# Feed-forward units of a hybrid decoder block on one core: from three seven-product and three plain units to four and one

## The chip, the cores and the metric

The kernel runs on one NeuronCore of a Trainium2 chip. The metric is the device time of one execution in microseconds; the median of three runs is shown. PE is TensorE (matmuls, transposes), DVE VectorE, ACT ScalarE, POOL GpSimd, SP the engine that issues most transfers.

## The reference

One decoder layer on 256 tokens of width 1024, all in float32. The change touches the feed-forward half alone:

```python
h = rms_norm(x, norm_ffn_pre_g[l])
f = (jax.nn.silu(h @ w_gate[l]) * (h @ w_up[l])) @ w_down[l]     # D_FF = 2816
x = x + rms_norm(f, norm_ffn_post_g[l])
```

## The kernel before

**Precision.** A float32 product is made of three matmuls of fp32r operands: each operand is split into a high part (`whi`: a ScalarE copy, L188) and a low part (`wlo`: source minus high, VectorE, L191), and `mm3` (L220 to L222) does high x high, high x low, low x high. Each weight tile (128 x 1024 elements, two rows of k for 512 columns) has one high and one low buffer out of a ring of five (`WB`), so the split of a tile waits until TensorE is through with the tile five places earlier.

**The feed-forward half.** The 2816 hidden columns are 22 chunks of 128 (`NFF`). Chunks 0 to 3 are computed first (`nat`). The other 18 go by `UNITS`:
- A plain unit R has two chunks: 8 x 2 x 3 matmuls of 512 columns (gate 256, up 256), two PSUM banks, 4 weight tiles. It ends with one group of four transposes.
- A seven-product unit W has four chunks. Two token halves t, two halves of k and the two matrices gate and up form 2 x 2 blocks, which are multiplied with seven products in place of eight (names "11", "T1", "T2", "22", "T3", "21", "T4"; each 4 x 3 = 12 matmuls of 512 columns, in two halves, one per weight tile). Its weights are sums: T1 and T3 are loaded and then a second matrix is added to them by an accumulating transfer on POOL's queue (L166); T2 and T4 are sums on VectorE (`job_add`, L271). The activations' sums (`S`, `s_step`) are made once. After its products, small VectorE and ScalarE operations put the two hidden tiles together (`q1` to `q7`).

**Transposes.** `f_T` (L997) turns a hidden tile (128 tokens x 512) into four 128 x 128 transposes in one PSUM bank, tag "t" (L1000), then copies the high part out (`fT`, ScalarE, L1005) and the low part (VectorE, L1007). The bank is free when the low part is done.

**Down terms.** For each chunk f a down-projection term `("d", f)` adds to the four output banks: 9 matmuls of 512 columns and 6 of 256, with one split tile of w_down (`dr`). A unit's slots are followed by the terms of the unit before it (`units_before`). The last four terms are the tail; their tiles lie in pages (`wextra`).

**What sets the order.** TensorE and SP take the order of the code; ScalarE, VectorE and POOL too in this half. `run` goes through the list of slots; before each slot it emits the split jobs that the slots ahead need (`granules_ahead`: up to four tiles, at most six slots), then the slot's matmuls, then what follows the slot. So in the lists of ScalarE and VectorE the splits for later slots stand between the small operations. Weights of W units lie in 12 pages (`free`), loaded in the order of first use (`page_order`) as soon as a page is released; other weights in a ring of seven raw buffers (`RB`). Each load is one instruction on SP's list.

```python
UNITS = [("R", 4), ("W", 6), ("R", 10), ("W", 12), ("R", 16), ("W", 18)]
head = slots_of("21", "b", A(0, 1), True, True, q2)
body = slots_of("11", "a", ...), [... ("T2", "a", ...), ("T1", "b", ...), ("T3", "a", ...), ("22", "b", ...), ("T4", "a", ...)]
return head + body[0], body[1], [f_T({1: lambda: st["f1"]}, f0, 4)]      # f_T of the first half ends body[1]
slots += a + zs[0:2] + (zs[2:] + b if i < len(UNITS) - 1 else b + zs[2:])
```

## Time and profile before

| | |
|---|---|
| median of 3 runs | 383.99 us (383.75 to 384.27) |
| profiled execution | 384.85 us, its span 383.1 us |
| TensorE matmul busy | 369.6 us, 96% of the span, 2212 instructions |
| TensorE weight loads busy | 322.8 us, 84% |
| VectorE busy | 298.1 us, 78%, 540 instructions |
| ScalarE busy | 234.2 us, 61%, 431 instructions |
| GpSimd busy | 47.1 us, 12% |
| transfers | 77.08 MB, mean 201 GB/s; mean granted TensorE clock 0.997 |

Matmuls overlap, so the distance from start to start tells what one costs, and a busy share near 100% does not say that no time is lost. A row of a timeline has start, duration, engine, line, operation, output<-inputs and, in brackets, the idle time before it with what released the engine. L numbers are lines of the kernel before.

### The profile page before, as it was taken

To read this page: it belongs to the slowest core of one execution; us is meant where nothing else is said; L and a number is where in the kernel's file an instruction comes from. 1 tells how busy PE (TensorE), PEld (TensorE's weight loads), DVE (VectorE), ACT (ScalarE), POOL (GpSimd) and SP (SyncE) were. 2 spreads that over 40 slices of the span, in tenths; PEclk is the share of its full clock that TensorE was granted. 3 is DMA by queue.
4 is the path that set the end of the run, shared out by engine and by line. 5 is a ranking of instruction groups with operands and counts; after the bars stand their busy time and mean duration, and the time that the engine had idled before them with its cause. 6 is when DMAs were issued, how large, how long until landed. Compare 5 with 4: busy or idle time off the path is not lost.

```text
span 383.1 us, 6164 instructions
## 1 busy us (share of the span) xinstructions
PE 369.6 (96%) x2212; PEld 322.8 (84%) x2212; DVE 298.1 (78%) x540; ACT 234.2 (61%) x431; POOL 47.1 (12%) x63
## 2 busy tenths in 40 slices
PE   6999999999999999999999999999999999999893
PEld 4799989999999999898888888887888877887683
DVE  3699797899978757789669886887588776877944
ACT  3985576778665865565467555684546853567721
POOL 0099600000001000000004010112001120000000
PEclk9999999999999999999999999999999999999998
DMA  6988646253654563577349999999958899300003
GB/s 204 388 255 322 198 137 201 70 164 113 215 153 128 193 192 125 188 215 248 107 120 318 299 401 274 386 282 360 297 147 221 239 347 300 129 0 0 3 0 110
DMA packets 42752, 77.08 MB, mean 201 GB/s; under 512 B 3281, under 2 KB 15586, under 8 KB 42722
## 3 DMA queue, kind: packets, MB, share of 16 engines
q1 hardware_dynamic: 39458, 70.40, 54.9%
q0 software_dynamic: 3264, 6.29, 9.1%
q8 instruction: 17, 0.28, 0.3%
q14 instruction: 13, 0.11, 0.1%
HBM read 75.64 MB, written 1.05 MB: 200 GB/s over the span
## 4 chain that ended last, share of the span: by engine, by line
PE 87%; DVE 5%; issue 2%; DMA 2%; ACT 1%; SPq 1%; DVEq 0%; POOLq 0%; ACTq 0%
PE acc L220 14%; PE acc L221 14%; PE acc L222 14%; PE s L220 9%; PE s L221 9%; PE s L222 9%; PE acc L620 5%; DVE wlo L191 2%; PE pv L221 2%; PE pv L222 2%; PE pv L220 2%; DMA xt<-in_x_dram 2%; ACT whi L188 1%; PE t L1000 1%; PE t L221 1%
## 5 line engine op out<-in xcount | busy, mean ns | idle before, releaser
L191 DVE TENSOR_TENSOR wlo<-wraw,whi 128x512 fp32r<-128x512 f32 (+1 forms) x137 | 116.7, 874 | 37.4 <-ACT whi L188 36.8
L188 ACT ACTIVATE whi<-wraw 128x512 fp32r<-128x512 f32 (+1 forms) x136 | 99.1, 766 | 36.9 <-PE acc L221 14.5
L220 PE MATMUL acc<-hTh,whi 128*128 128x256 f32 x256 | 73.1, 285 | 0.5 <-DVE q L559 0.5
L222 PE MATMUL acc<-hTh,wlo 128*128 128x256 f32 x256 | 71.8, 280 | 0.0
L221 PE MATMUL acc<-hTl,whi 128*128 128x256 f32 x256 | 71.8, 280 | 0.0
L191 DVE TENSOR_TENSOR wlo<-wpage,whi 128x1024 fp32r<-128x1024 f32 x42 | 49.9, 1222 | 12.1 <-ACT whi L188 12.0
L220 PEld LDWEIGHTS acc<-hTh,whi 128*128 128x128 f32 x256 | 48.3, 189 | 0.8 <-DVE q L559 0.7
L188 ACT ACTIVATE whi<-wpage 128x1024 fp32r<-128x1024 f32 x42 | 43.1, 1055 | 8.9 <-PE pv L222 6.3
L221 PEld LDWEIGHTS acc<-hTl,whi 128*128 128x128 f32 x256 | 48.3, 189 | 0.0
L222 PEld LDWEIGHTS acc<-hTh,wlo 128*128 128x128 f32 x256 | 48.2, 188 | 0.0
L220 PE MATMUL s<-whi,h2h 128*128 128x512 f32 x92 | 37.1, 404 | 0.6 <-DVE v L1086 0.6
L221 PE MATMUL s<-wlo,h2h 128*128 128x512 f32 x92 | 36.3, 395 | 0.0
L222 PE MATMUL s<-whi,h2l 128*128 128x512 f32 x92 | 36.3, 394 | 0.0
L166 POOL DMA_DIRECT2D wpage<-in_w_up_dram x12 | 14.6, 1220 | 106.7 <-DMA wpage<-in_w_up_dram 43.3
L220 PE MATMUL acc<-whi,fT 128*128 128x512 f32 x72 | 26.5, 369 | 0.0
L222 PE MATMUL acc<-whi,fT 128*128 128x512 f32 x72 | 26.2, 364 | 0.0
L221 PE MATMUL acc<-wlo,fT 128*128 128x512 f32 x72 | 26.2, 363 | 0.0
L220 PEld LDWEIGHTS s<-whi,h2h 128*128 128x128 f32 x92 | 17.3, 188 | 4.7 <-ACT wextra L188 1.0
L222 PEld LDWEIGHTS s<-whi,h2l 128*128 128x128 f32 x92 | 17.3, 188 | 4.3
L221 PEld LDWEIGHTS s<-wlo,h2h 128*128 128x128 f32 x92 | 17.3, 188 | 3.6
L220 PE MATMUL s<-whi,S 128*128 128x512 f32 x48 | 19.2, 399 | 0.3 <-DVE g L1071 0.2
L222 PE MATMUL s<-whi,S 128*128 128x512 f32 x48 | 19.0, 395 | 0.0
(268 smaller groups left out, 768.0 us busy)
## 6 DMA issues: line engine op xcount, KB each, us to landing
wraw<-in_w_in_dram SPq DMA_DIRECT2D x37, 512.0 KB, 4.7
wraw<-in_w_down_dram SPq DMA_DIRECT2D x22, 512.0 KB, 7.2
wpage<-in_w_gate_dram SPq DMA_DIRECT2D x18, 512.0 KB, 7.7
wpage<-in_w_up_dram SPq DMA_DIRECT2D x12, 512.0 KB, 7.4
wpage<-in_w_up_dram POOLq DMA_DIRECT2D x12, 512.0 KB, 9.9
wraw<-in_w_out_dram SPq DMA_DIRECT2D x8, 512.0 KB, 3.4
wraw<-in_w_gate_dram SPq DMA_DIRECT2D x12, 256.0 KB, 6.8
wraw<-in_w_up_dram SPq DMA_DIRECT2D x12, 256.0 KB, 7.0
```

Source lines behind the costliest of these rows:

```text
L166: nc.gpsimd.dma_start(r["tile"][:, :, c], v, accum_op=OP.add)
L188: nc.scalar.activation(hi, src, AF.Copy)
L191: nc.vector.tensor_tensor(lo, src, hi.bitcast(F32), op=OP.subtract)
L220: nc.tensor.matmul(dst, lh, rh, start=start, stop=False, **kw)
L221: nc.tensor.matmul(dst, lh, rl, start=False, stop=False, **kw)
L222: nc.tensor.matmul(dst, ll, rh, start=False, stop=stop, **kw)
L620: nc.tensor.matmul(acc[t], l[:, k, ts_], r, start=k == 0 and n == 0, stop=k == KT - 1 and n == 2)
L1000: nc.tensor.transpose(b[:, c:c + P], fvs[t]()[:, j * P:(j + 1) * P], ident)
```

## The change

`UNITS` becomes one plain unit (chunks 4, 5) and four seven-product units (6 to 9, 10 to 13, 14 to 17, 18 to 21). Within a W unit the products come as 11, T1, T2, 22, T3, 21, T4, with the down terms of the unit before placed between them (`plan_W`; the first W unit has two terms, the others four). T2 and T4 are summed in place in the page of 11, after the split that used it, so a unit needs ten pages and no page that isn't loaded. The banks of tag "s" become two tags "sa" and "sb" and rotate with "t" as `ring`; a W unit uses three. A unit's two groups of transposes are placed in the next unit, behind its first and its second product, both in that unit's third bank. The sums and gates are the generators `copy` (s1 of 11, v5 of T1, s2 of T2), `u1`, `u0`, `g0`, `g1`. Where two seven-product units meet is called a seam below.

```diff
--- before.py
+++ after.py
@@ -51,7 +51,7 @@
 RB = 7
 NWARM = 13
 NAT = 4
-UNITS = [("R", 4), ("W", 6), ("R", 10), ("W", 12), ("R", 16), ("W", 18)]
+UNITS = [("R", 4), ("W", 6), ("W", 10), ("W", 14), ("W", 18)]
 
 
 def _slopes():
@@ -98,8 +98,13 @@
 
         return const.tile([P, 1024], dt, tag=f"g{i}", name=name)
 
+    turn = []
+
     def ps(tag):
-        return psum.tile([P, 512], F32, tag=tag, bufs={"acc": 4, "s": 2}.get(tag, 1), name=tag)
+        if tag == "s":
+            turn.append(tag)
+            tag = "s" + "ab"[len(turn) % 2]
+        return psum.tile([P, 512], F32, tag=tag, bufs={"acc": 4}.get(tag, 1), name=tag)
 
 
 
@@ -272,17 +277,16 @@
             release(a, b)
         add_job(f)
 
-    def early_sums(f):
+    def raws_of_W(f):
 
         def two(*wk):
-
             return [raw_of([(slice(0, 512), rows(w, (k0 + 2 * i) * P, 2, f * P, 512)) for w, k0 in wk], 2, "page")
                     for i in range(2)]
 
-        b = wsum[f] = {"11": two((w_gate, 0)), "T3": two((w_up, 0), (w_up, 4)), "T2": two(),
-                       "21": two((w_gate, 4)), "T1": two((w_gate, 0), (w_up, 0)), "22": two((w_up, 4))}
-        b["T4"] = b["21"]
-        return [lambda i=i: job_add(b["T2"][i], b["11"][i], b["T3"][i]) for i in range(2)]
+        b = {"11": two((w_gate, 0)), "T1": two((w_gate, 0), (w_up, 0)), "T3": two((w_up, 0), (w_up, 4)),
+             "22": two((w_up, 4)), "21": two((w_gate, 4))}
+        b["T2"] = b["T4"] = b["11"]
+        return b
 
     def units_before(i):
 
@@ -302,36 +306,39 @@
                 add_job(lambda n=n: s_step(n))
         return [f]
 
...
+    def plan_W(i):
+
+        zs = [("z", f) for f in units_before(i)]
+        if len(zs) == 2:
+            return ["11", "T1", "T2", zs[0], "22", "T3"] + \
+                (["21", zs[1], "T4"] if i < len(UNITS) - 1 else ["21", "T4", zs[1]])
+        return ["11", "T1", "T2", zs[0], "22", zs[1], "T3", zs[2], "21"] + \
+            ([zs[3], "T4"] if i < len(UNITS) - 1 else ["T4", zs[3]])
 
     for ui, (kind, f0) in enumerate(UNITS):
-        ds = [lambda i=i: job_split(("d", i), dr[i]) for i in units_before(ui)]
         if kind == "R":
             rr = [raw_of([(slice(0, 256), rows(w_gate, 2 * kc * P, 2, f0 * P, 256)),
                           (slice(256, 512), rows(w_up, 2 * kc * P, 2, f0 * P, 256))], 2) for kc in range(4)]
...
+            todo = [lambda kc=kc: job_split(("r", f0, kc), rr[kc]) for kc in range(4)]
             if ui == 0:
                 uns = [lambda kc=kc: job_split(("un", kc), nr["un", kc]) for kc in range(1, 4)]
-                todo = uns[0:1] + s_jobs(0) + uns[1:2] + s_jobs(1) + uns[2:3] + s_jobs(2, 3, 4, 5) + rs[0:2] + \
-                    s_jobs(6) + rs[2:3] + s_jobs(7, 8) + rs[3:4] + braid(ds, ad[0:4])
-                rest = ad[4:]
-            else:
-                todo = braid(rs + ds, ad)
-                rest = []
+                todo = uns[0:1] + s_jobs(0) + uns[1:2] + s_jobs(1) + uns[2:3] + s_jobs(2, 3, 4, 5) + todo[0:2] + \
+                    s_jobs(6) + todo[2:3] + s_jobs(7, 8) + todo[3:4]
+            todo += [lambda i=i: job_split(("d", i), dr[i]) for i in units_before(ui)]
         else:
-            b = wsum[f0]
-            sp = {n: [lambda n=n, i=i: job_split((n, f0, i), b[n][i]) for i in range(2)]
-                  for n in ("11", "21", "22", "T1", "T2", "T3", "T4")}
-            t4 = [lambda i=i: job_add(b["T4"][i], b["T2"][i], b["21"][i]) for i in range(2)]
-            todo = sp["21"] + sp["11"] + rest[0:1] + ds[0:1] + t4[0:1] + rest[1:2] + ds[1:2] + t4[1:2]
-            for n in ("T2", "T1", "T3", "22", "T4"):
-                todo += sp[n]
+            b, todo = raws_of_W(f0), []
+            for n in plan_W(ui):
+                if n[0] == "z":
+                    todo.append(lambda f=n[1]: job_split(("d", f), dr[f]))
+                    continue
+                for i in range(2):
+                    if n == "T1":
+                        todo.append(lambda i=i: job_split(("T1", f0, i), b["T1"][i]))
+                        todo.append(lambda i=i: job_add(b["T2"][i], b["11"][i], b["T3"][i]))
+                    else:
+                        todo.append(lambda n=n, i=i: job_split((n, f0, i), b[n][i]))
+                    if n == "21":
+                        todo.append(lambda i=i: job_add(b["T4"][i], b["T2"][i], b["21"][i]))
         for f in todo:
             f()
     for f in range(NFF - NTAIL, NFF):
@@ -990,7 +997,7 @@
 
         return fT[f, t]
 
-    def f_T(fvs, f0, n, tag="t"):
+    def f_T(fvs, f0, n, tag):
 
         def pe():
             b = ps(tag)
@@ -1047,71 +1054,64 @@
             mm3(bank, a(k), [v[:, j, :] for v in w], start=start and k == 0, stop=stop and k == 3,
                 skip_group_check=True)
 
-    def unit_W(f0):
-        st = {}
+    def unit_W(ui, f0, ring):
+
+        st, made = {}, {}
+        banks = dict(zip("acb", ring))
 
         def bank(n):
             if n not in st:
-                st[n] = ps("s")
+                st[n] = ps(banks[n])
             return st[n]
 
-        def slots_of(n, bk, a, start, stop, post):
-            return [dict(pe=lambda kp=kp: block(bank(bk), a, n, f0, kp, start, stop), need=[((n, f0, kp), 0)],
+        def slots_of(n, bk, a, start, post):
+            return [dict(pe=lambda kp=kp: block(bank(bk), a, n, f0, kp, start, True), need=[((n, f0, kp), 0)],
                          post=[lambda: active.append(post())] if kp else []) for kp in range(2)]
 
...
+        def copy(n, tag, bk, **kw):
+            def f():
+                made[n] = work.tile([P, 512], F32, tag=tag, name=n, **kw)
+                nc.scalar.activation(made[n], st[bk], AF.Copy)
+                yield
+            return f
+
+        def u1():
+            nc.vector.tensor_tensor(made["v5"], made["v5"], st["a"], op=OP.subtract)
+            yield
+
+        def u0():
+            u = made["s2"]
+            nc.vector.tensor_tensor(u, st["c"], u, op=OP.subtract)
+            yield
+
+        def g0():
+            g = made["s1"]
+            nc.vector.tensor_tensor(g, st["b"], g, op=OP.add)
             yield
             nc.scalar.activation(g, g, AF.Silu, scale=rs2[:, 0:1])
...
+            yield
+            u = made["s2"]
+            nc.vector.tensor_tensor(u, u, g, op=OP.mult)
+
+        def g1():
+            g = made["g1"] = work.tile([P, 512], F32, tag="e", name="g1", bufs=4)
             nc.scalar.activation(g, st["a"], AF.Silu, scale=rs2[:, 1:2])
             yield
...
+            nc.vector.tensor_tensor(g, g, made["v5"], op=OP.mult)
+
+        how = {"11": ("a", A(0, 0), True, copy("s1", "ph0", "a", bufs=1)),
+               "T1": ("c", R_(0), True, copy("v5", "pl0", "c", bufs=1)),
+               "T2": ("a", R_(1), False, copy("s2", "e", "a", bufs=4)), "22": ("c", R_(3), False, u0),
+               "T3": ("a", R_(2), False, u1), "21": ("b", A(0, 1), True, g0), "T4": ("a", A(1, 1), False, g1)}
+        sl = [s for n in plan_W(ui) for s in (z_slots("d", n[1], f_of, NFF - 1) if n[0] == "z" else slots_of(n, *how[n]))]
+        return sl, [lambda tag: f_T({0: lambda: made["s2"]}, f0, 4, tag), lambda tag: f_T({1: lambda: made["g1"]}, f0, 4, tag)]
+
+    def unit_R(f0, ring):
         st = []
 
         def pe(kc, t):
             if not st:
-                st.extend([dict(b=ps("s")), dict(b=ps("s"))])
+                st.extend(dict(b=ps(n)) for n in ring[0:2])
             w = W(("r", f0, kc))
             for j in range(2):
                 k = 2 * kc + j
@@ -1126,7 +1126,7 @@
 
         sl = [dict(pe=lambda kc=kc, t=t: pe(kc, t), need=[(("r", f0, kc), 0)],
                    post=[lambda t=t: active.append(done(t))] if kc == 3 else []) for kc in range(4) for t in range(NT)]
-        return sl, [f_T({t: (lambda t=t: st[t]["f"]) for t in range(NT)}, f0, 2)]
+        return sl, f_T({t: (lambda t=t: st[t]["f"]) for t in range(NT)}, f0, 2, ring[2])
 
     def nat_slots():
         def pe(kc, t):
@@ -1151,16 +1151,20 @@
     for t in range(NT):
         slots[t]["post"] = [lambda t=t: nat_silu(t)]
         slots[t - NT]["post"] = [lambda t=t: nat_mul(t)]
-    left = [f_T({t: lambda t=t: fgs[t]}, 0, 4, "pv" if t else "t") for t in range(NT)]
+    left = [lambda _, t=t: f_T({t: lambda: fgs[t]}, 0, 4, "pv" if t else "t") for t in range(NT)]
     for i, (kind, f0) in enumerate(UNITS):
-        zs = [s for f in units_before(i) for s in z_slots("d", f, f_of, NFF - 1)]
+        ring = [("sa", "sb", "t")[(i + j) % 3] for j in range(3)]
         if kind == "R":
-            sl, tr = unit_R(f0)
-            slots += sl[0:2] + left + sl[2:] + zs[0:3] + tr + zs[3:]
-            left = []
+            zs = [s for f in units_before(i) for s in z_slots("d", f, f_of, NFF - 1)]
+            sl, tr = unit_R(f0, ring)
+            sl += zs[0:3] + [tr] + zs[3:]
+            new = []
         else:
-            a, b, left = unit_W(f0)
-            slots += a + zs[0:2] + (zs[2:] + b if i < len(UNITS) - 1 else b + zs[2:])
+            sl, new = unit_W(i, f0, ring)
+        if left:
+            sl = sl[0:2] + [left[0](ring[2])] + sl[2:4] + [left[1](ring[2])] + sl[4:]
+        slots += sl
+        left = new
     tail = list(range(NFF - NTAIL, NFF))
     t0 = z_tail("d", tail, f_of, 0, NFF - 1)
     t1 = z_tail("d", tail, f_of, 1, NFF - 1)
@@ -1184,7 +1188,9 @@
     t1[1]["post"] = [lambda: norm3(1)]
     t1[2]["post"] = [lambda: pn[1][0](1)]
     t1[3]["post"] = [lambda: finish(1)]
-    slots += t0[0:1] + left + t0[1:] + t1
+    ring = [("sa", "sb", "t")[(len(UNITS) + j) % 3] for j in range(3)]
+    slots[-1:] = [left[0](ring[2])] + slots[-1:]
+    slots += t0[0:1] + [left[1](ring[2])] + t0[1:] + t1
     run(slots, granules_ahead(slots, WB - 1, 6))
     order.__exit__(None, None, None)
 
```

What the change moves is seen in the lists of ScalarE and VectorE. Names: `whi<-wraw` is the high part of a down weight (or of a plain unit's weight), `whi<-wpage` that of a seven-product unit's weight; `wlo` the low parts; `wpage<-wpage` a sum of `job_add`.

VectorE at the seam behind a seven-product unit, before (chunks 6 to 9, followed by a plain unit): the multiply of the second half f1, then the two low parts of fT.

```order
L191 TENSOR_TENSOR wlo<-wraw,whi 128x1024 x2
L1099 TENSOR_TENSOR f_3298<-f_3298,v_3232 128x512
L1007 TENSOR_TENSOR fT<-t,fT 128x512
L191 TENSOR_TENSOR wlo<-wraw,whi 128x1024
L271 TENSOR_TENSOR wpage<-wpage 128x1024
L191 TENSOR_TENSOR wlo<-wraw,whi 128x1024
L1007 TENSOR_TENSOR fT<-t,fT 128x512
```

And now (chunks 14 to 17, followed by 18 to 21), from the low part of T1's first half on:

```order
L196 TENSOR_TENSOR wlo<-wpage,whi 128x1024
L276 TENSOR_TENSOR wpage<-wpage 128x1024
L196 TENSOR_TENSOR wlo<-wpage,whi 128x1024
L276 TENSOR_TENSOR wpage<-wpage 128x1024
L196 TENSOR_TENSOR wlo<-wpage,whi 128x1024
L1100 TENSOR_TENSOR g_3868<-g_3868,v_3653 128x512
L196 TENSOR_TENSOR wlo<-wpage,whi 128x1024
L196 TENSOR_TENSOR wlo<-wraw,whi 128x1024
L1014 TENSOR_TENSOR fT<-sa,fT 128x512
L196 TENSOR_TENSOR wlo<-wpage,whi 128x1024 x2
L1014 TENSOR_TENSOR fT<-sa,fT 128x512
```

The splits and sums of T1 and T2 and one down weight's low part now stand ahead of fT's first low part.

ScalarE in the plain unit (chunks 4 and 5), before: both copies fT of the first chunks, then the first two down weights.

```order
L188 ACTIVATE whi<-wraw 128x1024
L1005 ACTIVATE fT<-t 128x512
L1005 ACTIVATE fT<-pv 128x512
L188 ACTIVATE whi<-wraw 128x1024 x2
L1123 ACTIVATE fr<-s,rs_2746 128x256
```

And now:

```order
L193 ACTIVATE whi<-wraw 128x1024
L1012 ACTIVATE fT<-t 128x512
L193 ACTIVATE whi<-wraw 128x1024
L1012 ACTIVATE fT<-pv 128x512
L193 ACTIVATE whi<-wraw 128x1024
L1123 ACTIVATE fr<-sa,rs_2748 128x256
```

The first down weight's high part went ahead of the second copy fT.

VectorE at the end of the last unit, now: `g0` (`s_3893<-sa`) is the gate's sum, the `wextra` are the four tail weights, `s_3958` becomes the half f0, `g_4109` the half f1.

```order
L196 TENSOR_TENSOR wlo<-wraw,whi 128x1024
L196 TENSOR_TENSOR wextra<-wraw,wextra 128x1024 x2
L1089 TENSOR_TENSOR s_3893<-sa,s_3893 128x512
L196 TENSOR_TENSOR wextra<-wraw,wextra 128x1024 x2
L1094 TENSOR_TENSOR s_3958<-s_3958,s_3893 128x512
L1100 TENSOR_TENSOR g_4109<-g_4109,v_3927 128x512
L1014 TENSOR_TENSOR fT<-sb,fT 128x512
```

Two tail weights stand ahead of the gate's sum, two between it and the multiply.

## Rows read from the trace of the kernel before

**Rows 1.** TensorE's timeline (start, us, line, operation): plain unit and first down term.

```profile
213.74 0.39 PE L220 MATMUL s<-whi,h2h 128*128 128x512 f32 x1
...
218.12 0.40 PE L220 MATMUL s<-whi,h2h 128*128 128x512 f32 x1
...
225.60 0.40 PE L222 MATMUL s<-whi,h2l 128*128 128x512 f32 x1
225.83 0.40 PE L220 MATMUL acc<-whi,fT 128*128 128x512 f32 x1
...
228.59 0.39 PE L220 MATMUL acc<-whi,fT 128*128 128x512 f32 x1
```

**Rows 2.** Busy times in one stretch: PE, PEld, DVE, ACT, POOL, clock, DMA, GB/s.

```profile
196.00:346.00 150.00, 148.09 (x709) 121.76 (x709) 118.35 (x128) 90.39 (x109) 16.19 (x13) 1.00 0.86 263
```

**Rows 3.** TensorE's timeline at the first seam (the second, at 316.66, reads alike).

```profile
265.45 0.40 PE L222 MATMUL s<-whi,h2l 128*128 128x512 f32 x1
266.80 0.66 PE L1000 MATMUL t<-ident,f 128*128 128x128 f32 x4 [0.95 <-DVE fT L1007]
267.21 0.48 PE L220 MATMUL s<-whi,h2h 128*128 128x512 f32 x1
```

**Rows 4.** ScalarE's and VectorE's timelines at the same seam.

```profile
262.65 0.69 ACT L1097 ACTIVATE f<-s,rs 128x512 f32<-128x512 f32 x1 [3.14 <-PE s L222]
263.24 1.05 ACT L188 ACTIVATE whi<-wraw 128x1024 fp32r<-128x1024 f32 x1
264.19 0.59 ACT L1005 ACTIVATE fT<-t 128x512 fp32r<-128x512 f32 x1
...
264.32 1.23 DVE L191 TENSOR_TENSOR wlo<-wraw,whi 128x1024 fp32r<-128x1024 f32 x1 [1.91 <-ACT whi L188]
265.46 0.69 DVE L1099 TENSOR_TENSOR f<-f,v 128x512 f32<-128x512 f32 x1
266.06 0.68 DVE L1007 TENSOR_TENSOR fT<-t,fT 128x512 fp32r<-128x512 f32 x1
```

**Rows 5.** TensorE's timeline in the last unit: before T4, and before its first transposes.

```profile
357.20 0.39 PE L222 MATMUL s<-whi,S 128*128 128x512 f32 x1
358.17 0.47 PE L220 MATMUL s<-whi,h2h 128*128 128x512 f32 x1 [0.57 <-DVE v L1086]
...
360.81 0.39 PE L222 MATMUL s<-whi,h2l 128*128 128x512 f32 x1
361.76 0.63 PE L1000 MATMUL t<-ident,f 128*128 128x128 f32 x4 [0.56 <-DVE f L1092]
```

**Rows 6.** Timelines, splits in a row: VectorE (three) and ScalarE (two).

```profile
243.21 3.49 DVE L191 TENSOR_TENSOR wlo<-wpage,whi 128x1024 fp32r<-128x1024 f32 x3
...
231.09 2.00 ACT L188 ACTIVATE whi<-wpage 128x1024 fp32r<-128x1024 f32 x2
```

**Rows 7.** ScalarE's and POOL's timelines in the plain unit; DMA queues 212:218, rate 224:230.

```profile
207.45 1.27 ACT L1147 ACTIVATE fgs<-s,rs 128x512 f32<-128x512 f32 x2 [2.06 <-POOL rs L440]
...
219.42 1.06 ACT L188 ACTIVATE whi<-wraw 128x1024 fp32r<-128x1024 f32 x1 [1.16 <-DMA wraw<-in_w_down_dram]
221.06 1.06 ACT L188 ACTIVATE whi<-wraw 128x1024 fp32r<-128x1024 f32 x1 [0.58 <-DMA wraw<-in_w_down_dram]
...
205.44 1.98 POOL L440 TENSOR_TENSOR rs<-rs_e,mhalf 128x2 f32<-128x2 f32 x1
209.70 1.23 POOL L166 DMA_DIRECT2D wpage<-in_w_up_dram  x1 [2.29 <-ACT whi L188]
...
q0 software_dynamic: 323, 0.63, 56.5%
q1 hardware_dynamic: 326, 1.15, 51.5%
...
DMA packets 1167, 2.36 MB, mean 394 GB/s; under 512 B 74, under 2 KB 122, under 8 KB 1167
```

More of the change, by code (lines that the diff above doesn't have):

```diff
@@ L303, in s_jobs @@
         return [f]
-    def braid(a, b):
-        n, o = len(a), []
-        for i in range(n):
-            o += a[i:i + 1] + b[len(b) * i // n:len(b) * (i + 1) // n]
-        return o
+    def plan_W(i):
[5 more added lines that the diff above has]
+            ([zs[3], "T4"] if i < len(UNITS) - 1 else ["T4", zs[3]])
     for ui, (kind, f0) in enumerate(UNITS):
-        ds = [lambda i=i: job_split(("d", i), dr[i]) for i in units_before(ui)]
         if kind == "R":
@@ L1069, in q1 @@
             yield
-            g = st["g0"] = work.tile([P, 512], F32, tag="e", name="g0", bufs=4)
-            nc.vector.tensor_tensor(g, st["b"], s1, op=OP.add)
+        def g0():
+            g = made["s1"]
+            nc.vector.tensor_tensor(g, st["b"], g, op=OP.add)
             yield
             nc.scalar.activation(g, g, AF.Silu, scale=rs2[:, 0:1])
-        def q6():
-            st["s2"] = work.tile([P, 512], F32, tag="ph0", name="s2", bufs=1)
-            nc.scalar.activation(st["s2"], st["a"], AF.Copy)
@@ L1095, in q4 @@
-        def q4():
-            g = st["f1"] = work.tile([P, 512], F32, tag="e", name="f1", bufs=4)
+            u = made["s2"]
+            nc.vector.tensor_tensor(u, u, g, op=OP.mult)
+        def g1():
+            g = made["g1"] = work.tile([P, 512], F32, tag="e", name="g1", bufs=4)
             nc.scalar.activation(g, st["a"], AF.Silu, scale=rs2[:, 1:2])
             yield
-            nc.vector.tensor_tensor(g, g, st["v5"], op=OP.mult)
-        head = slots_of("21", "b", A(0, 1), True, True, q2)
@@ L1102, in unit_W @@
-        body = slots_of("11", "a", A(0, 0), True, True, q1), [
-            s for x in (("T2", "a", R_(1), False, True, q6), ("T1", "b", R_(0), True, True, q5),
-                        ("T3", "a", R_(2), False, True, q7), ("22", "b", R_(3), False, True, q3),
-                        ("T4", "a", A(1, 1), False, True, q4)) for s in slots_of(*x)]
-        body[1].append(f_T({0: lambda: st["f0"]}, f0, 4))
-        return head + body[0], body[1], [f_T({1: lambda: st["f1"]}, f0, 4)]
-    def unit_R(f0):
+            nc.vector.tensor_tensor(g, g, made["v5"], op=OP.mult)
```

19 lines of the change are left out of this document (removed).

## The prediction, made before the changed kernel was run

> **What bounds the kernel now.** I read four views, in this order. First the busy times by stage: between 196 and 346 us TensorE is busy 148.09 of 150 us and VectorE 118.35 [rows 2]. So TensorE's matmuls set the time of the feed-forward stage, and VectorE has a fifth of it free. Second, TensorE's timeline, where the reader should look at starts and not at durations. The plain unit's matmuls start at 218.12 and, 32 later, at 225.60, which is 0.2338 us each; a down-projection term runs from 225.83 to 228.59, 2.76 us [rows 1]. Half a product (6 matmuls) is thus 1.40 us. Third, TensorE's few gaps. Twice, where a seven-product unit is followed by a plain one, the unit's second group of transposes waits for the VectorE read that empties the same bank: from 265.45 to 266.80 there are 1.35 us where 0.23 belong, a loss of 1.12 [rows 3]. In the last unit two more gaps lose 0.97 - 0.23 = 0.74 and 0.95 - 0.23 = 0.72 [rows 5]. Fourth, what those waits hang on: in the trace ScalarE and VectorE take their lists in order, and at the seam a weight's high part, the copy fT, the same weight's low part and only then the low part of fT follow one another [rows 4].
>
> So there are 2.24 us at two seams and 1.46 us at the end to be won besides the matmuls, and each depends on what stands ahead of a short operation in two lists.
>
> **The change, part by part.**
>
> *Matmuls.* Three seven-product units (84 matmuls each) and three plain ones (48) make 396; four and one make 384. Twelve fewer at 0.2338 us [rows 1] are **-2.81 us**, all on TensorE's path. Down terms and transposes keep their number.
>
> *More splits and sums.* A seven-product unit has 14 weight tiles to split for four chunks, plain units 8: six more splits, and four more sums. On VectorE successive ones start (3.49 - 1.22)/2 = 1.135 us apart [rows 6], so it gets 11.4 us more in a stage where it had about 30 free [rows 2]. As a total that is hidden; where it stands ahead of something TensorE waits for, it is not. ScalarE gets 6 x 0.95 [rows 6] and had more free.
>
> *Units that now follow one another.* At each of the three seams the old unit's two groups of transposes go into one bank, with the first and second product of the new unit around them. Count from the end of T4 (0); a and b are a product's halves. TensorE's 11 ends at 2.80, transposes take 0.41 [rows 3], T1 ends at about 6.0, and there the second group wants the bank. It is free once VectorE's low part of fT is through. The hidden cost is the order: ScalarE has the high part of T2's second half, which waits for the second in-place sum, *ahead* of the copies s1 and fT; VectorE has the low part of a down weight ahead of fT's low part.
>
> Seams two and three: the buffer for T1's first half comes free at -2.80, its high part runs -2.75 to -1.70, and VectorE then has low T1a, sum, low T1b, sum, starting at -1.65, -0.52, 0.62, 1.75, the last ending at 2.97 (1.22 long [rows 6], and about 0.03 to 0.05 per hand-over, as from 264.29 to 264.32 in [rows 4]). Then ScalarE: high T2b at 3.0, s1 at 3.95, fT at 4.45, high of the down weight 4.95 to 6.0. Then VectorE: its low part at 6.05, fT's low part at 7.2 for 0.68. The transposes start near 7.95: **1.9 us** lost, twice. Seam one: the first seven-product unit has only two down terms between its products, so VectorE comes later. From -12.85 on (the term before 22 ends at -14.0, then a high part) it has nine long and four short operations in a row, 9 x 1.135 + 4 x 0.60 [rows 4, 6] = 12.6, and starts on T1a at -0.2 and not -1.65; the whole chain shifts by 1.5: **3.4 us**. Together 7.2 against the 2.24 of before: **+4.96**. From below: three waits of the present 1.12 (+1.1); from above: all three like the first (+8.0).
>
> *The end.* The gaps of [rows 5] go, since T4 no longer comes right behind the product whose bank it needs. What is late next: the last unit's first half f0 needs the gate's sum, its silu and a multiply, and the tail's four down weights stand in between. From T4's end: the down weight's buffer is free at -5.6, VectorE does its low part and two of the tail from -4.45, so the sum for the gate starts at -1.05; silu to 0.4; two further tail weights on ScalarE to 2.35, their low parts on VectorE to 3.7; the multiply ends at 4.4. TensorE wants f0 at 1.4, after half a down term. **3.05** lost against 1.46: **+1.6** (from 0 to +2.6).
>
> *The first down terms.* The first seven-product unit now fetches T1 and T3 early, where it fetched T3 and needed no load for T2: two plain transfers and two accumulating ones more stand ahead of the down weights d0 and d1. Already now ScalarE waits for these: d0 lands at 219.42, d1 at 221.06 [rows 7]. While an accumulating transfer runs, its queue takes 56.5% of the DMA engines' time and the plain queue gets 1.15 MB in 6 us; without one the rate is 394 GB/s [rows 7]. A 512 KB transfer (0.524 MB) thus takes 2.74 us or 1.33. The present accumulates, the second issued at 209.70 [rows 7], end about when d1 lands; two more follow at once. So I take d1 two slots of 2.74 later: 226.5. The new list puts the copy of fT's second bank behind d0's high part and its low part behind d1's low part: 226.5 + 1.06 + 1.22 + 0.68 and hand-overs is 229.5. TensorE's sixth matmul of d0 needs that low part at 225.83 + 5 x 0.2338 = 227.0 [rows 1]. **+2.5**. From below: two slots of 1.33 give 223.7 and 226.8, no wait. From above: d1 only after both added accumulates, 2 x 0.524 MB at 0.63 MB in 6 us = 10 us past 221: +7. The middle is taken because these slots lie among transfers of just this kind.
> The same accumulates stand on POOL's list: the power for rs2 now follows two and not one, so it starts about 1.23 (one issue) + 1.33 (one more load) later than 205.44 [rows 7]. Behind it come ScalarE's silu and the split of the plain unit's first weight: 207.45 + 1.27 + 2.56 + 1.06 + 1.22 = 213.6, and TensorE needs its low part one matmul after 213.74 [rows 1, 7]. Costed at nothing; if that load is later, so is TensorE, one for one.
>
> [...]
>
> *Sum.* -2.81 + 4.96 + 1.6 + 2.5 = **+6.2 us**. Against the profiled execution, 384.85 (span 383.1 and 1.75 around it), that is 391.1; that execution lies 0.86 above the median of the runs, 383.99, so for the median I say **390.2**.
>
> **The rivals.**
>
> *TensorE alone decides (faster).* The mechanism: VectorE keeps ahead at the seams, as its free fifth suggests, and fT's low part ends within the 2.8 us that the product between two groups lasts. It decides at that point: about 1.9 us (3.4 at the first seam) earlier than I count. Then the seam waits vanish: -2.81 - 2.24 + 1.6 + 2.5 = -1.0, 383.0; if the down weights also come in time and the end costs what it does now, -5.05, 378.9; about 381 between them. For it: plain units' single groups wait for nothing today. Against it: at today's seams VectorE was idle 1.91 us right before [rows 4] and the transposes still waited.
> [...] This trace has TensorE waiting at the seams with VectorE 79% busy.
>
> *The DMA queues become the bound.* Added are 2 x 1.33 and 4 accumulates at 3.39 us of engine time per 0.63 MB [rows 7], 2.8 each: 14 us. Before, their mean busy share is 0.86 over the 150 us [rows 2], so 21 us are free, but usable only where pages come free in time. If the last accumulate of each next unit comes 2.7 us (one slot) late, the second sum and all behind it shift at every seam: +8, 398.
>
> *The change does less than it says.* Excluded: the instruction lists show the 384 matmuls and the new order.
>
> **How the numbers follow.** Forecast (seam, end and start waits of this size within a few us): 0.59, 384.8 to 395. TensorE alone: 0.20. DMA bound: 0.13. Waits that just eat the gain: 0.08. A measurement of this kernel can tell about 0.2% (0.8 us) from no change. Faster 0.20, same 0.08, slower 0.72. The range goes down to 382.5, near the lower ends together (-2.81 + 1.1 = -1.7), leaving out the better part of the first rival, and up to 396, short of the DMA rival.
>
> **What would show it.** Right: three waits of the second transpose group for fT's low part, 1.9 to 3.4 us, the longest at the first seam; about 2.5 us of TensorE idle near 227 with ScalarE waiting for a w_down transfer just before; one gap of 3 us before the last unit's first group; no gap of [rows 5]'s kind before T4. Wrong: VectorE's fT done before the second group is due; d1 landing before 224; or TensorE waiting inside a unit for a sum or an accumulate, which would be the DMA rival.

## The result, and the profile after

The changed kernel takes **394.31 us** (median of four runs; 384.06 for the kernel before beside it), a ratio of 1.0263 (95%: 1.0243 to 1.0283). Measured a second time, with the experiments below, it took 396.32 us (393.79 to 397.94) against 384.12, ratio 1.0312 (1.026 to 1.0363). The prediction was 390.2 in a range of 382.5 to 396: the first median lies inside it, the second 0.3 above. The profiled run of the first measurement was a slow one (401.25 us) and is left out of the ratio, so the profile shown here is the second measurement's, an execution of 397.94 us (span 396.2), the longest of its four. Against the profiled execution of before, 384.85, that is 13.1 us more.

The page's busy times (us, share of the span, instructions):

```profile
PE 371.7 (94%) x2200; PEld 325.0 (82%) x2200; DVE 312.0 (79%) x551; ACT 243.5 (61%) x438; POOL 51.3 (13%) x67
```

The stretch that answers to [rows 2], with the same columns (busy us of PE, PEld, DVE, ACT, POOL, then granted clock, DMA share, GB/s):

```profile
196.00:346.00 150.00, 138.64 (x642) 113.15 (x641) 124.05 (x129) 95.18 (x111) 20.54 (x17) 0.98 0.93 280
```

TensorE was idle for 11.4 of 150 us where it had been for 1.9, although VectorE is busy 0.83 of the stretch and not more. The clock column reads 0.98 where it read 1.00. TensorE's timeline names the places (start, us, line, operation; in brackets the idle time and what ended it); each pair is the matmul before a gap and the instruction behind it:

```profile
225.11 0.40 PE L225 MATMUL acc<-whi,fT 128*128 128x512 f32 x1
...
226.04 0.40 PE L226 MATMUL acc<-wlo,fT 128*128 128x512 f32 x1
228.76 0.50 PE L227 MATMUL acc<-whi,fT 128*128 128x512 f32 x1 [2.32 <-DVE fT L1014]
...
271.77 0.39 PE L227 MATMUL sa<-whi,S 128*128 128x512 f32 x1
277.49 1.12 PE L1007 MATMUL sb<-ident,g 128*128 128x128 f32 x4 [5.33 <-DVE fT L1014]
...
312.53 0.66 PE L1007 MATMUL t<-ident,g 128*128 128x128 f32 x4 [2.00 <-DVE fT L1014]
...
346.28 0.66 PE L1007 MATMUL sa<-ident,g 128*128 128x128 f32 x4 [1.99 <-DVE fT L1014]
...
370.18 0.40 PE L227 MATMUL acc<-whi,fT 128*128 128x512 f32 x1
373.73 1.09 PE L1007 MATMUL sb<-ident,s 128*128 128x128 f32 x4 [3.15 <-DVE s L1094]
```

These are the first down term, the three seams and the end, the five places that the prediction named; the gap of [rows 5] ahead of T4 is gone. In the first down term ScalarE waits for both down weights (d0 and d1, its timeline), and fT's low part, for which TensorE waits, stands on VectorE behind d1's low part:

```profile
222.09 1.06 ACT L193 ACTIVATE whi<-wraw 128x1024 fp32r<-128x1024 f32 x1 [5.01 <-DMA wraw<-in_w_down_dram]
...
225.79 1.06 ACT L193 ACTIVATE whi<-wraw 128x1024 fp32r<-128x1024 f32 x1 [2.15 <-DMA wraw<-in_w_down_dram]
...
228.02 0.68 DVE L1014 TENSOR_TENSOR fT<-pv,fT 128x512 fp32r<-128x512 f32 x1
```

At the second seam ScalarE and VectorE show the order that it counted on, and the first seam differs in one thing, a transfer (timelines of ScalarE and VectorE):

```profile
307.63 1.06 ACT L193 ACTIVATE whi<-wpage 128x1024 fp32r<-128x1024 f32 x1 [1.22 <-DVE wpage L276]
308.60 0.58 ACT L1074 ACTIVATE s<-sa 128x512 f32<-128x512 f32 x1
309.07 0.59 ACT L1012 ACTIVATE fT<-t 128x512 fp32r<-128x512 f32 x1
309.55 1.06 ACT L193 ACTIVATE whi<-wraw 128x1024 fp32r<-128x1024 f32 x1
...
309.17 1.22 DVE L196 TENSOR_TENSOR wlo<-wpage,whi 128x1024 fp32r<-128x1024 f32 x1
310.64 1.23 DVE L196 TENSOR_TENSOR wlo<-wraw,whi 128x1024 fp32r<-128x1024 f32 x1 [0.25 <-ACT whi L193]
311.79 0.68 DVE L1014 TENSOR_TENSOR fT<-t,fT 128x512 fp32r<-128x512 f32 x1
...
271.26 1.23 DVE L276 TENSOR_TENSOR wpage<-wpage 128x1024 f32<-128x1024 f32 x1 [1.76 <-DMA wpage<-in_w_up_dram]
```

The high part of T2b waits for the in-place sum (L276), s1 and fT's copy stand behind it; on VectorE the low parts of T2b and of a down weight stand ahead of fT's low part, which ends at 312.47, and the transposes start 0.06 later. At the first seam that sum itself waits 1.76 us for an accumulating load.

What no step of the prediction had is behind the gaps (stretches of the same execution, columns as above):

```profile
228.00:234.00 6.00, 5.24 (x21) 4.50 (x22) 4.79 (x7) 3.42 (x4) 0.00 (x0) 0.72 1.04 394
...
277.00:281.00 4.00, 3.51 (x12) 3.00 (x13) 2.34 (x3) 1.59 (x4) 2.41 (x2) 0.58 0.75 190
...
312.00:316.00 4.00, 3.47 (x17) 2.93 (x18) 2.80 (x4) 2.56 (x4) 0.00 (x0) 1.00 1.03 190
...
346.00:350.00 4.00, 3.72 (x18) 3.13 (x19) 2.80 (x4) 2.75 (x4) 0.00 (x0) 1.00 0.41 131
...
373.00:380.00 7.00, 6.27 (x24) 5.44 (x24) 1.88 (x3) 0.60 (x1) 0.00 (x0) 0.54 0.01 2
```

and on TensorE's timeline behind the first seam:

```profile
278.83 0.63 PE L226 MATMUL t<-wlo,S 128*128 128x512 f32 x1
279.26 0.63 PE L227 MATMUL t<-whi,S 128*128 128x512 f32 x1
279.69 0.63 PE L225 MATMUL t<-whi,S 128*128 128x512 f32 x1
```

Behind the gaps of 2.32, 5.33 and 3.15 us the granted clock reads 0.72, 0.58 and 0.54 over the stretches shown, and matmuls start up to 0.43 us apart in place of 0.234 for some 3 to 6 us; behind those of 2.00 and 1.99 it reads 1.00. Summed over these matmuls and transposes (start to start, less what the same step takes at a clock of 1.00, 0.234 for 512 columns and about 0.115 for 256) that is about 5.4 us.

So the 13.1 us are, by the prediction's own terms in this execution: matmuls -2.81 (x2200 against x2212); first down term +2.49; seams 5.49 + 2.16 + 2.15 against 2.24, +7.56; the end 3.32 against 1.46, +1.86; two small gaps of before in its last unit (0.38 and 0.24) gone, -0.6; lower clock +5.4. Sum +13.9, 0.8 more than measured. Nearly all of that is a start outside the sum: this execution had come to the plain unit 0.70 us earlier than that of before (first matmul at 213.04 against 213.74 [rows 1]).

### The profile page after: what moved, and what is told of

Same layout as the page of the kernel before. It is cut to its first block, busy times and chain, and to the rows that moved or that the text cites. A ratio compares the mean times of both kernels' runs of the same rounds, so it can differ in the third digit from the quotient of the medians.

```text
span 399.5 us, 6168 instructions
## 1 busy us (share of the span) xinstructions
PE 374.8 (94%) x2200; PEld 327.2 (82%) x2200; DVE 312.2 (78%) x551; ACT 243.5 (61%) x438; POOL 51.1 (13%) x67
## 4 chain that ended last, share of the span: by engine, by line
PE 76%; DMA 10%; DVE 6%; issue 3%; ACT 3%; SPq 0%; DVEq 0%; POOLq 0%; ACTq 0%
PE acc L225 13%; PE acc L227 13%; PE acc L226 13%; PE acc L627 5%; DMA wraw<-in_w_down_dram 5%; PE sb L226 3%; PE sb L225 3%; PE sb L227 3%; DMA wpage<-in_w_up_dram 3%; DVE wlo L196 2%; PE t L226 2%; PE t L225 2%; PE t L227 2%; PE sa L225 2%; PE sa L226 2%
## 5 line engine op out<-in xcount | busy, mean ns | idle before, releaser
L196 DVE TENSOR_TENSOR wlo<-wraw,whi 128x512 fp32r<-128x512 f32 (+1 forms) x129 | 107.1, 853 | 30.7 <-ACT whi L193 30.2
L193 ACT ACTIVATE whi<-wraw 128x512 fp32r<-128x512 f32 (+1 forms) x128 | 91.2, 749 | 44.3 <-PE acc L226 14.5
L196 DVE TENSOR_TENSOR wlo<-wpage,whi 128x1024 fp32r<-128x1024 f32 x56 | 68.2, 1222 | 17.1 <-ACT whi L193 16.8
L193 ACT ACTIVATE whi<-wpage 128x1024 fp32r<-128x1024 f32 x56 | 59.1, 1060 | 32.8 <-PE pv L227 17.8
L171 POOL DMA_DIRECT2D wpage<-in_w_up_dram x16 | 19.5, 1252 | 114.0 <-DVE wlo L196 57.7
L276 DVE TENSOR_TENSOR wpage<-wpage 128x1024 f32<-128x1024 f32 x16 | 19.5, 1219 | 1.9 <-DMA wpage<-in_w_up_dram 1.9
L227 PEld LDWEIGHTS acc<-whi,fT 128*128 128x128 f32 x72 | 14.2, 198 | 4.6 <-DVE fT L1014 2.2
L672 ACT ACTIVATE e<-e,nmx 128x256 f32<-128x256 f32 (+1 forms) x32 | 14.3, 447 | 5.8 <-DVE nmx L669 5.4
L225 PEld LDWEIGHTS acc<-whi,fT 128*128 128x128 f32 x72 | 14.2, 198 | 3.0
L226 PEld LDWEIGHTS acc<-wlo,fT 128*128 128x128 f32 x72 | 14.2, 198 | 2.9
L527 POOL TENSOR_SCALAR bias<-nd 128x256 f32<-128x256 f32 x12 | 13.0, 1081 | 0.7
```

What stands on the lines that cost most here:

```text
L171: nc.gpsimd.dma_start(r["tile"][:, :, c], v, accum_op=OP.add)
L193: nc.scalar.activation(hi, src, AF.Copy)
L196: nc.vector.tensor_tensor(lo, src, hi.bitcast(F32), op=OP.subtract)
L225: nc.tensor.matmul(dst, lh, rh, start=start, stop=False, **kw)
L226: nc.tensor.matmul(dst, lh, rl, start=False, stop=False, **kw)
L227: nc.tensor.matmul(dst, ll, rh, start=False, stop=stop, **kw)
```

## The experiments

Each is an edit of the changed kernel unless it says otherwise. Ratios are to the kernel before, run beside it.

| run | us, median | ratio, 95% interval |
|---|---|---|
| e1_after (unaltered) | 396.32 | 1.0312, 1.026 to 1.0363 |
| e2_late | 392.17 | 1.0213, 1.0169 to 1.0256 |
| e3_tail | 389.39 | 1.0163, 1.0115 to 1.0211 |
| e4_fill | 390.47 | 1.0175, 1.0124 to 1.0226 |
| e5_mix | 389.00 | 1.0112, 1.0072 to 1.0152 |
| e8_noacc | 391.40 | 1.0173, 1.0136 to 1.021 |
| e11_low | 388.13 | 1.0095, 1.0064 to 1.0127 |
| e6_both | 382.22 | 0.9951, 0.9925 to 0.9976 |
| e7_22 | 384.39 | 1.0004, 0.9988 to 1.0019 |
| e9_caps | 379.15 | 0.9881, 0.9856 to 0.9906 |
| e10_mix | 381.59 | 0.9926, 0.9913 to 0.9939 |
| e12_noacc | 376.55 | 0.9821, 0.9792 to 0.985 |

**e1_after.** 

> The changed kernel again, unaltered, for a profile to set beside the others: 393.8 to 394.6 us. Theory (order of the lists): TensorE waits for fT's low part before the second transposes of each seam, 2 us at seams two and three and 3.4 or more at the first, 2 us in the first down term and 3 us before the last unit's first transposes. Rival (the DMA queues): the first seam's wait is longer than 3.4 us by what ScalarE and VectorE wait there for accumulating page loads, 2 us or more.

Its profile is the one above. The first seam waits 5.33 us, 1.9 more than the 3.4 of the order alone, with 1.76 us of it VectorE's wait for an accumulating load: both theories have a part there, though the load's is short of the 2 us that its theory asked for. The median lies 2 us above what was expected.

**e8_noacc: the accumulating loads.** 

> The changed kernel with its sixteen accumulating transfers left out (T1 and T3 are loaded with one matrix and not the sum of two, so the products are other numbers); all else as it was. Order of the lists: the seams still wait 3.4, 2.0 and 2.0 us and the end 3.1; the first down term's wait goes, because d0 and d1 land earlier: 388 to 391.5 us, with little spread between runs. DMA rival: the first seam's wait falls below 2.5 us as well, 385 to 387.5 us.

```diff
-        b = {"11": two((w_gate, 0)), "T1": two((w_gate, 0), (w_up, 0)), "T3": two((w_up, 0), (w_up, 4)),
+        b = {"11": two((w_gate, 0)), "T1": two((w_gate, 0)), "T3": two((w_up, 0)),
```

391.40 us. The first seam on TensorE's timeline, and on ScalarE's the high parts of d0 and d1:

```profile
271.17 1.11 PE L1007 MATMUL sb<-ident,g 128*128 128x128 f32 x4 [3.48 <-DVE fT L1014]
...
216.71 1.06 ACT L193 ACTIVATE whi<-wraw 128x1024 fp32r<-128x1024 f32 x1
...
219.94 1.05 ACT L193 ACTIVATE whi<-wraw 128x1024 fp32r<-128x1024 f32 x1
```

The first seam waits 3.48 us with no accumulating load in the kernel, the other two 2.00 and 1.99, the end 3.15: these waits are order. The first term waits for nothing: d0 and d1 are split at 216.71 and 219.94 (222.09 and 225.79 with the accumulates), and both splits follow other work and not a transfer. So the late landing was the accumulating transfers' doing; as their bytes are gone too, this run does not tell whether it is that they accumulate or that they are sixteen transfers more. The runs spread by 2.5 us (389.67 to 392.21), where little had been expected.

**e11_low: one edit of order.** 

> The changed kernel with one edit: fT's low part is issued at once behind its copy, ahead of the down weight's low part that follows. Order of the lists, one VectorE operation of 1.14 us less ahead of it: the first down term's wait goes, seams two and three wait 0.9 us in place of 2.0, the first 2.4 (4.2 where an accumulating load is late there), the end 3.15 as before: 387.5 to 391 us. Rival (down weights land too late, whatever the order): the first term still waits 1.5 us or more, 391 to 393.5 us.

```diff
             next(th)
-            active.append(th)
+            next(th, None)
```

388.13 us (386.65 to 391.1), 6 to 8 us less than the two medians of the unaltered kernel, from one line. Seams one and two on TensorE's timeline:

```profile
273.53 1.12 PE L1007 MATMUL sb<-ident,g 128*128 128x128 f32 x4 [3.60 <-DVE fT L1014]
...
308.25 0.66 PE L1007 MATMUL t<-ident,g 128*128 128x128 f32 x4 [0.53 <-DVE fT L1014]
```

Seams two and three fall from 2.00 to 0.53 and the first from 5.33 to 3.60, somewhat more than the 1.14 expected: VectorE's wait of 0.25 us for that down weight's high part, seen above at 310.64, no longer stands ahead of fT either. At the first seam a sum waits 1.67 us for an accumulating load here too, so the two are alike in that. The first term's wait is gone although ScalarE still waits 1.04 us for d1's transfer (its split starts at 224.98, not at 219.94 as without accumulates): it takes a late transfer *and* a list that puts fT's low part behind it. A wait of 1.16 us for the plain unit's multiply, behind the third down weight, is what comes next there.

**e2_late: the seams.** 

> The second transposes of each seam stand behind the product T2 and not ahead of it, so their bank is wanted 2.8 us later, with fT's low part issued at once. Order of the lists: the waits of seams two and three (2.0 each) go, the first shrinks to under 2.7, and the stretches at the lower granted clock behind them go too: 383 to 387 us. DMA rival: what TensorE no longer waits for at the first seam it waits for in T2 or behind it, because sums and accumulating loads are late there: only the 4 us of seams two and three come back, 389 to 391 us.

```diff
-            sl = sl[0:2] + [left[0](ring[2])] + sl[2:4] + [left[1](ring[2])] + sl[4:]
+            n = 6 if i > 1 else 4
+            sl = sl[0:2] + [left[0](ring[2])] + sl[2:n] + [left[1](ring[2], n == 6)] + sl[n:]
...
```

392.17 us, above both ranges. The wait for the bank goes, but the down term right behind the transposes now waits for their copies: 0.47 and 0.83 us at seams two and three. At the first seam the wait moves into T2 (1.66 us for the copy s1, behind a sum that waits 1.38 us for an accumulating load) and into the down term (1.08 and 0.83), which is where the rival looked for it. The down term was my slip: half a down term serves both row tiles, so only 0.7 us lie between the transposes and the first use of f1, less than copy and low part take (0.59 and 0.68 us at the second seam above). So here the transposes can be moved back only so far as their copies still fit ahead of the down term.

**e3_tail: the end.** 

> The tail's four down weights are split later: the first two behind the last unit's gate sum, the other two behind the copies of f0. Order of the lists: the 3.1 us before the last unit's first transposes fall to under 0.5 and the half-rate matmuls behind them go: 389.5 to 391.5 us. Rival (VectorE has too much to do at the end, whatever the order): TensorE then waits as long for the low parts of the third and fourth weight, 393.5 to 395 us.

```diff
-    run(slots, granules_ahead(slots, WB - 1, 6))
+    far = granules_ahead(slots, WB - 1, 6)
+    n3 = len(slots) - len(t1) - len(t0) + 1
...
+        if i < n3 - 2:
+            a = min(a, n3 - 1 - i)
+        if i < n3 - 7:
+            a = min(a, n3 - 3 - i)
+        return a
+    run(slots, near)
```

389.39 us (387.72 to 392.35), 0.1 below the range of the order theory. VectorE's timeline at the end, where the multiply (L1094) now stands ahead of two of the tail's four splits and the transposes wait for nothing:

```profile
362.59 2.35 DVE L196 TENSOR_TENSOR wextra<-wraw,wextra 128x1024 fp32r<-128x1024 f32 x2
364.86 0.69 DVE L1094 TENSOR_TENSOR s<-s,s 128x512 f32<-128x512 f32 x1
...
368.17 2.36 DVE L196 TENSOR_TENSOR wextra<-wraw,wextra 128x1024 fp32r<-128x1024 f32 x2 [0.26 <-ACT wextra L193]
```

The mean granted clock of this execution is 0.991, against 0.979 in that of e1_after. The rival (VectorE too busy in any order) is out. In this execution no sum waited for an accumulate at the first seam, and TensorE waited 3.50 us there.

**e4_fill: the clock.** 

> Dummy matmuls that add zeros to an accumulator stand where TensorE waits: 22 of 128x256 ahead of the first seam's second transposes (2.4 us at 0.11 each), 14 at the other two seams, 24 ahead of the last unit's first transposes; they are shorter than the waits, so no wait ends later. If the granted clock falls because TensorE stood idle, it stays at 1.00 behind these places, and the matmuls there start 0.234 and not 0.43 us apart: 2 to 4 us come back, 390 to 392.5 us. If the clock falls for another reason (the chip's load), nothing changes: 394 us, or up to 1 us more.

```diff
+    def fill(n):
+        def pe():
+            for _ in range(n):
+                nc.tensor.matmul(zb[0][0][2][:, 0:2 * P], warm[:, 0:P], warm, start=False, stop=False,
+                                 skip_group_check=True)
+        return dict(pe=pe, need=[], short=True)
...
```

390.47 us: lowest and highest run are 388.89 and 393.48 against 393.79 and 397.94, 4.5 to 4.9 us less, for matmuls *added*. TensorE's timeline at the first seam:

```profile
268.65 2.58 PE L1153 MATMUL acc<-warm 128*128 128x256 bf16 x22
273.03 0.66 PE L1007 MATMUL sb<-ident,g 128*128 128x128 f32 x4 [1.80 <-DVE fT L1014]
273.44 0.48 PE L225 MATMUL t<-whi,S 128*128 128x512 f32 x1
273.76 0.39 PE L226 MATMUL t<-wlo,S 128*128 128x512 f32 x1
```

and two stretches of the same execution, columns as above:

```profile
272.00:282.00 10.00, 8.97 (x44) 7.52 (x45) 7.65 (x9) 6.72 (x8) 3.61 (x3) 1.00 0.96 240
...
370.00:380.00 10.00, 10.00 (x55) 8.49 (x55) 4.41 (x9) 3.08 (x9) 0.57 (x1) 1.00 0.15 54
```

The product still has to wait (to 273.03, 4.4 us past the end of T1, longer than the 3.6 after which e8_noacc dropped to 0.66 between 271 and 276), but the clock stays at 1.00 behind it and behind the end. So at these two places the lower clock hung on TensorE's idle time: 0.58 and 0.54 behind the gaps of e1_after, 1.00 in the two stretches here.

Not all of the gain is clock. The two profiled executions, 397.94 and 388.89, are 9.05 us apart. About 3.8 of that is the clock behind the first seam and the end, where the dummies stand. About 3.0 is the first down term, which has no dummies: it waited 1.01 us here in place of 2.32, and its clock stayed at 1.00. The first seam waits 1.1 less, the end 0.7, and the plain unit started 0.5 earlier. And the edit did one thing that it was not meant to do: the dummies are slots, so the splits that run some slots ahead moved too. At the end two of the tail's splits went behind the gate's sum, two behind the multiply, as in e3_tail, and the transposes stand behind the dummies alone (VectorE's and TensorE's timelines):

```profile
363.56 0.69 DVE L1094 TENSOR_TENSOR s<-s,s 128x512 f32<-128x512 f32 x1
...
364.65 2.79 PE L1153 MATMUL acc<-warm 128*128 128x256 bf16 x24
367.28 0.60 PE L1007 MATMUL sb<-ident,s 128*128 128x128 f32 x4
```

So there they cost 2.6 us that TensorE need not have waited, and the expectation that no wait ends later missed.

**e5_mix: the old units under the new code.** 

> The changed code (three banks in turn, spread down terms, its order of products) with the old mix of units, three and three, 396 matmuls and no seam between two seven-product units. If the loss sits in the seams and in what they do to the clock: 383 to 386.5 us, with the first down term and the end still waiting (2 and 3 us). Rival (the rest of the new code costs it, whatever the mix): 390 us or more.

```diff
-UNITS = [("R", 4), ("W", 6), ("W", 10), ("W", 14), ("W", 18)]
+UNITS = [("R", 4), ("W", 6), ("R", 10), ("W", 12), ("R", 16), ("W", 18)]
```

389.00 us, between the two ranges; one of the four runs took 397.23. TensorE's timeline in its last unit:

```profile
356.46 0.47 PE L225 MATMUL t<-whi,h2h 128*128 128x512 f32 x1 [1.15 <-ACT wextra L193]
...
365.16 0.76 PE L1007 MATMUL t<-ident,s 128*128 128x128 f32 x4 [4.28 <-DVE s L1094]
```

No seam waits, as expected, but with two down terms in the last unit the tail's splits cost more, 4.28 + 1.15 us, and the first term 1.30. So with the old mix too the new code is 4.8 us slower than before, although the two seam waits of before are gone; I had put first term and end at 4.1 together. That fits neither theory as it stood.

**e6_both: three edits of order together** (those of e11_low and e3_tail, and the second transposes behind the first half of T2). 

> Three edits of order, no work added or left out: fT's low part is issued at once behind its copy, everywhere; the seams' second transposes stand half a product later (behind the first half of T2); the tail's splits stand as in the run on the tail. Order of the lists: first down term 2 us less, seams two and three wait for nothing, the first 1 to 2.8 us, the end under 0.5: 380 to 383.5 us, faster than before. Rival (VectorE and the DMA queues are short at the first seam and in the first term): waits turn up at the next half products instead, 385 to 388 us.

382.22 us, as the order theory had it: the kernel with four seven-product units is faster than before once the lists are put right. What is left on TensorE's timeline is 4.9 us: 2.5 of it at the first seam (1.24 for the copy s1 behind T2b's high part, 0.95 in the down term) and 1.3 for the plain unit's multiply. At the first seam a sum still waits 0.79 us for an accumulating load.

**e7_22: T2 later.** 

> As the run of the three edits, and in each seven-product unit the product 22 stands ahead of T2, whose two sums move with T2: VectorE has two long operations fewer ahead of the seam's fT. If VectorE's load at the seams is what is left, this takes the first seam's wait below 0.5 us: 378.5 to 381.5 us. If the accumulating loads are what is left, T3's pages come at another time but no fewer, and it gains less than 1 us on the run of the three edits.

```diff
-            return ["11", "T1", "T2", zs[0], "22", "T3"] + \
+            return ["11", "T1", "22", zs[0], "T2", "T3"] + \
...
```

384.39 us, 2.2 *more* than e6_both. Product 22 now follows T1 in the same bank and waits for ScalarE's copy v5, 0.69 us in each of the four units, as here on TensorE's timeline:

```profile
271.76 0.50 PE L225 MATMUL sa<-whi,S 128*128 128x512 f32 x1 [0.69 <-ACT v L1074]
```

A miss: I had freed VectorE and not looked at who shares the bank.

**e9_caps: how far splits run ahead** (on top of e6_both, with the second transposes of seams two and three back behind T1). 

> The three edits of order together with a limit on how far splits run ahead: at each seam the high part of T2's second half goes behind the copies s1 and f0, the parts of 22 go behind f1's, and in the first plain unit the third down weight goes behind the unit's own silu and multiply; the second transposes go back to their place behind T1 at seams two and three. Order of the lists: the 1.1 us before the plain unit's transposes, the 1.2 us before T2 and the 0.3 to 1.0 us in the down terms behind the seams go: 379 to 380.8 us. Rival (the first seam is short of VectorE time and of data, whatever the order): what is taken from one wait there comes back at the next half product, 381.3 to 382.5 us.

```diff
...
+                caps.extend((s, zs[4]) for s in (sl[6], sl[7], zs[0]))
+            elif i > 1:
+                caps.extend((s, sl[5]) for s in (sl[0], sl[1], l0))
+                caps.extend((s, sl[8]) for s in (sl[3], sl[4], l1))
...
```

**379.15 us, 1.2% faster than before.** Its profiled execution took longer, 382.19 us, with a clock of 0.83 between 10 and 20 us, ahead of the feed-forward half, and two late accumulating loads at the first seam (ScalarE waits 2.93 us for one, VectorE 1.66 us for the other). Every gap of over 0.12 us on TensorE there from 196 us on:

```profile
268.22 0.66 PE L1007 MATMUL sb<-ident,s 128*128 128x128 f32 x4 [1.67 <-ACT g L1098]
...
272.92 0.51 PE L226 MATMUL t<-wlo,S 128*128 128x512 f32 x1 [1.01 <-DVE wlo L196]
...
275.25 0.50 PE L226 MATMUL t<-wlo,S 128*128 128x512 f32 x1 [0.22 <-DVE wlo L196]
```

**e10_mix and e12_noacc** go after what is left. The first is e9_caps with the edit of e5_mix, the second e9_caps with that of e8_noacc. 

> The same kernel with the old mix of units, three and three: 396 matmuls and not 384, no seam between seven-product units. If the waits are order alone, the mix is worth its twelve matmuls, 2.8 us (2.3 to 3.2 between the two kernels): 381.8 to 384 us. Rival (seven-product units in a row load VectorE and the DMA queues so that part of the 2.8 us is lost again): the two differ by less than 1.8 us.

> The kernel with the limit on the splits, its accumulating transfers left out (T1 and T3 are loaded with one matrix, so the products are other numbers). If accumulating loads are what is left at the first seam: its waits fall below 0.5 us in all and the runs lie within 0.6 us of each other, 377 to 378.7 us. If VectorE's time is what is left: within 0.5 us of the kernel with them, 378.8 to 380 us.

With the old mix the same code takes 381.59 us, 0.2 below what was expected: the two mixes differ by 2.44 us, near the twelve matmuls' 2.81. Neither is free of waits, though: in the profiles e10_mix has one of 1.15 us in its last unit and e9_caps those of the first seam, so the 2.44 is not the matmuls alone. With the accumulates left out e9_caps takes 376.55 us, 0.45 below the range. Three of four runs lie within 0.14; the fourth, which is the profiled one, took 378.92, again with a clock of 0.83 between 10 and 20 us. From 196 us on its TensorE loses 0.18 us at one place and not more than 0.11 at any other. The stretch of [rows 2], without the accumulates:

```profile
196.00:346.00 150.00, 150.00 (x718) 123.57 (x717) 136.20 (x145) 103.97 (x125) 0.70 (x1) 1.00 0.66 228
```

VectorE is busy 0.91 of that stretch and holds nobody up. So the last 2.6 us of e9_caps, which its profile has all at the first seam, go with the accumulating loads; as in e8_noacc, bytes and kind of transfer went together.

## Why the prediction was right in kind and short in size

*Matmuls, -2.81.* Held in the count (2200 against 2212); the two mixes differ by 2.44 us once the lists are in order, some other waits included.

*Seams, 3.4, 1.9 and 1.9.* The mechanism was right, as traced above: 3.48, 2.00 and 1.99 without accumulates, and moving one low part ahead takes 1.5 to 1.7 us from each. The first seam's term was mis-sized as run, 5.33 in place of 3.4, where a page lands late, as it did in both profiled executions of the unaltered kernel. That is a piece of the DMA rival, whose late transfer it is; it came at one seam, not at all three.

*The end, 3.05.* Measured 3.15, and gone with the reordering of the tail's splits.

*The first down term, +2.5.* Measured 2.49 (2.32 of wait). d1's high part started at 225.79, where I had its landing at 226.5; without the accumulates (e8_noacc) it started at 219.94, 5.85 us earlier. So the late landing was theirs, as I had it; by what rule the queues share the DMA engines no run shows. The mechanism held as far as that; that the size came out so exactly is luck, for in other profiles with the same lists up to there the wait was 2.12 (e2_late), 1.62 (e3_tail) and 1.01 us (e4_fill).

*POOL's power for rs2, 0.* Held: ScalarE's silu did start later (208.49 against 207.45 [rows 7]), but TensorE has no gap in the plain unit; the first down term starts at 225.11, where before it started at 225.83 [rows 1], and the 0.72 between them is the 0.70 by which this execution had come to the plain unit earlier.

*What failed* is the sum's silent premise that TensorE's matmuls cost 0.2338 us wherever they stand. I priced each wait as its length. The lower clock behind the longer ones adds about 5.4 us in the profiled execution; with the late accumulate's 1.9 that is 7.3, against the 6.8 us by which the execution lies above the 391.1 of the prediction's sum. The clock's part does not hang on the late load: in e8_noacc, which has none, the matmuls behind the first seam and the end add about 4 us.

*The rivals.* That TensorE alone decides fell at the seams, but a time near its 381 (378.9 to 383.0) is what the change gives once the lists are in order (379.15). That waits just eat the gain would have needed them half as long.

## What to carry to other kernels

Price a wait on TensorE as its length plus what the clock gives up behind it (about 5.4 us in all in e1_after), and look for the second part in the trace: the length of the wait did not tell it here (behind the same 3.15 us matmuls ran slower for 5.9 us in e1_after and for 3.7 in e2_late). Where an engine takes its list in order, a short operation that frees a bank goes ahead of the long prefetch work; here that order was worth 15 to 17 us, the clock's part included, from 394.3 or 396.3 to 379.15, and the mix of units 2.4. Of the 5.0 us by which e9_caps beats the kernel before, half is thus not the mix: the new code with the old mix (e10_mix) is already 2.55 us faster. And a longer lookahead is not a safe default: at all five places a split prefetched for later stood in front of something due. Last, an edit that adds slots where a lookahead counts slots moves other work too, as e4_fill did.

## What the hardware showed that was not expected

- The granted clock fell within the kernel, behind TensorE's own gaps: 0.72, 0.58 and 0.54 in the stretches behind waits of 2.32, 5.33 and 3.15 us, and 0.66 and 0.50 behind 3.50 and 3.60 us in e3_tail (272 to 277) and e11_low (273 to 279), while 2.00 and 1.99 left it at 1.00 there, and so did 2.12 in e2_late (228 to 234). The length of the gap alone does not decide: behind the same 3.15 us at the end matmuls ran slower for 5.9 us in e1_after and for 3.7 in e2_late (0.76, first line below, against 0.54), and in the first measurement's profiled run (401.25 us) the clock fell behind 2.02 us at the second seam (second line). With dummy matmuls in the gap it stayed at 1.00 (e4_fill, 272 to 282 and 370 to 380).

```profile
369.00:376.00 7.00, 6.74 (x30) 5.81 (x31) 1.41 (x3) 1.20 (x2) 0.00 (x0) 0.76 0.01 2
...
314.00:318.00 4.00, 3.83 (x12) 3.15 (x13) 2.56 (x4) 1.82 (x3) 0.00 (x0) 0.57 0.99 215
```

- Runs of one kernel spread by 4 us (393.79 to 397.94) where the kernel before, beside it, spread by 0.8 (383.73 to 384.52). With lists in order the spread was 1.7 (e6_both), and without accumulates but with the lists as they were 2.5 (e8_noacc). With both mended three of four runs lie within 0.14 and the fourth 2.4 above them. So neither late transfers nor the lists alone make the spread, and what does is not shown; the longest runs of e9_caps and e12_noacc, both profiled, have the lower clock between 10 and 20 us.
